# A streamed logsumexp: GpSimd weighs and folds heads of the last units, a fourth head for its bias add in the middle stages, ScalarE's sums of the last tile at the end, and exp(bias) of six heads in PSUM

## The chip, the core and the metric

The kernel runs on one core of a Trainium2 chip. The time is that of the device in microseconds (us); five runs of the kernel before have a median of 329.27 us (328.9 to 329.38). TensorE (PE in the profile), VectorE (DVE), ScalarE (ACT), GpSimd (POOL) and SyncE (SP, which issues the loads) each work through their own queue in order, and wait for one another by semaphores.

## What is computed

x has the shape 8 x 2048 x 2048, 134 MB in float32. Its last axis is split into 8 heads of 256 elements. A bias per head and element is added, and the logsumexp over the 256 elements of each head is written twice (every row of a head is repeated).

```python
x_heads = x.reshape(B, S, H, Dh).transpose(0, 2, 1, 3)
x_heads = x_heads + bias[None, :, None, :]
x_tiled = np.repeat(x_heads, 2, axis=2)
mx = x_tiled.max(axis=-1, keepdims=True)
lse = mx.squeeze(-1) + np.log(np.exp(x_tiled - mx).sum(axis=-1))
```

Both kernels leave out the maximum: they sum exp(x + bias), or exp(x) times exp(bias), and take the logarithm.

## The kernel before, in words

**Tiles and buffers.** The 16,384 rows of x make 64 tiles of 256 rows: 128 partitions with K = 2 rows each, 2 MB a tile. Nine buffers in SBUF hold tiles (NBUF). A load of tile t + 9 is issued by SyncE when all last uses of tile t are done. Most tiles come in one load, the later ones in halves (one of the two rows of each partition, 1 MB), and the two halves of the last tile in three pieces each (LAST_CUTS). "62k1" below means tile 62, second half.

**Three ways for the bias.** For a head, the sum of exp(x + bias) comes about in one of three ways:

- by TensorE: a matmul with bf16 parts of the bias (L193, three rows) and one of x with the identity (L204) add up in a PSUM bank. ScalarE takes exp with its own sum as a side output (`sum_biased`, L223). This costs ScalarE an instruction and an accumulator read for each head.
- by GpSimd: it adds the bias in place (`g_add`, L242), ScalarE takes exp in place (L248), and VectorE sums (L265, in `later`).
- by weights: ScalarE takes exp(x) in place (L248), and VectorE multiplies by exp(bias) and sums. This is either one multiply for several heads (L258) with the reduce at L265, or one custom instruction and an accumulator read for each head (`weigh`, L276), which can start as soon as exp is done.

**Stages.** STAGES gives each tile a mode: `pe` heads go by TensorE, heads from `g0` on by GpSimd, those between by weights. `late` says that the weighted heads wait for GpSimd and use L258; otherwise they are weighed as soon as they have landed. BULK (tiles 0 to 48) has 2 heads by TensorE, 2 by weights, 4 by GpSimd. MIXED (49 to 60, from 57 in halves) has 1, 4 and 3. PROMPT (61 to 63) has 2 by TensorE and 6 by weights; GpSimd has nothing to do there.

**Order.** All engines follow an order written out by hand in the main loop (`tc.manual_schedule`). At each unit of work (a tile, a half or a piece) the loop first issues TensorE's matmuls and GpSimd's add, then what was put off from the unit before: `for_pool` (ScalarE's exp and VectorE's reduce of the heads that GpSimd prepared, and the load of tile t + 9), then the exp of this unit, then `for_pe` (ScalarE's sums of the TensorE heads, in PROMPT put off by one unit), then the weighings. PSUM holds exp(bias) of heads 1 to 4 (w_ps, two banks), five banks for TensorE's sums (ps) and one for transposes. exp(bias) of heads 5 to 7 is in SBUF (w_sb).

**End.** Sums go into R (seven batches) and R_last. After each batch TensorE transposes it (`finish`, L293) and ScalarE takes Ln (L303). One store (L307) writes seven batches; it is issued after all loads. `finish_last` (L314, L320, L321) does the same for the last batch.

Of the kernel before, what the change touches and what calls it, by code (L numbers as in the profile page):

```python
# [19 lines left out]

BULK = dict(pe=2, g0=4, late=True)
MIXED = dict(pe=1, g0=5, late=False)
PROMPT = dict(pe=2, g0=8, late=False)

STAGES = [(0, BULK, False), (49, MIXED, False), (57, MIXED, True), (61, PROMPT, True)]

LAST_CUTS = [[0, 512, 1280, 2048], [0, 512, 1536, 2048]]


@with_exitstack
def kernel(
# [6 lines left out]
    nc = tc.nc  # L40
    P = nc.NUM_PARTITIONS
    B, S, D = x.shape
    H, Dh = bias.shape
    assert D == H * Dh and S % (P * K) == 0
    NBLK = S // (P * K)
    T = B * NBLK
    CPE = 2 * Dh
    MM = 512

    W0, G0, W1 = Dh, 4 * Dh, 5 * Dh  # L50

# [7 lines left out]
    w_sb = sb.tile([P, D - W1], F32, name="w_sb")  # L59
# [9 lines left out]
    res = sb.tile([H * NBLK, B - 1, P, K, 2], F32, name="res")  # L69
    res_last = sb.tile([P, P, 2], F32, name="res_last")  # L70
    xts = [sb.tile([P, K, D], F32, name=f"xt{i}") for i in range(NBUF)]
    w_ps = pp.tile([P, W1 - W0], F32, name="w_ps")
    ps = [pp.tile([P, MM], F32, name=f"ps{i}") for i in range(5)]
    tpair = pp.tile([P, 2, K, P], F32, name="tpair")
    tps = [tpair[:, i] for i in range(2)]

    def mode_of(t):
        return [m for t0, m, _ in STAGES if t0 <= t][-1]

    def halves_of(t):  # L80
        return [s for t0, _, s in STAGES if t0 <= t][-1]

    def pieces(t):

        if not halves_of(t):
            return [(0, K, 0, D)]
        cuts = [[0, D]] * K if t < T - 1 else LAST_CUTS
        return [
            (k, k + 1, c0, c1) for k in range(K) for c0, c1 in zip(cuts[k], cuts[k][1:])
        ]  # L90

    def rows_of(t):

# [79 lines left out]
    for c in range(W0, W1, MM):  # L173
# [5 lines left out]

    n_ps = [0]  # L180

    def add_bias(m, t, k0, k1):


        n = m["pe"] * Dh
        xt = xts[t % NBUF]
        step = MM // n
        groups = [(k, min(k + step, k1)) for k in range(k0, k1, step)]
        got = []
        for ka, kb in groups:  # L190
            p = ps[n_ps[0] % len(ps)]
            n_ps[0] += 1
            nc.tensor.matmul(  # L193
                p[:, 0 : (kb - ka) * n],
                lhsT=ones3,
                rhs=each_row(b3, 0, n, kb - ka),
                start=True,
                stop=False,
            )
            got.append([p[:, k * n : (k + 1) * n] for k in range(kb - ka)])  # L200
        rows = []
        for (ka, kb), views in zip(groups, got):
            p = views[0]
            mm = nc.tensor.matmul(  # L204
                bass.AP(
                    tensor=p.tensor,
                    offset=p.offset,
                    ap=[p.ap[0], [1, (kb - ka) * n]],
                ),
                lhsT=ident,  # L210
                rhs=xt[:, ka:kb, 0:n],
                start=False,
                stop=True,
            )
            on_x(t, mm, [loads[t, k0, 0]])
            rows += [(v, mm) for v in views]
        return rows

    def sum_biased(m, t, k, p, mm, sums):
# [11 lines left out]
    def each_row(src, c, n, k_rows):  # L231

        return bass.AP(
            tensor=src.tensor,
            offset=src.offset + c,
            ap=[src.ap[0], [0, k_rows], [1, n]],
        )

    def g_add(m, t, k0, k1):
        c = m["g0"] * Dh  # L240
        v = xts[t % NBUF][:, k0:k1, c:D]
        add = nc.gpsimd.tensor_tensor(  # L242
            out=v, in0=v, in1=each_row(b_rep, c - G0, D - c, k1 - k0), op=ALU.add
        )
        return on_x(t, add, [loads[t, k0, 0]])

    def exp_inplace(t, v, after):
        return on_x(t, nc.scalar.activation(out=v, in_=v, func=ACT.Exp), [after])  # L248
# [23 lines left out]

    def weigh(t, v, h, dst, after):
        c = h * Dh
        w = w_ps[:, c - W0 : c - W0 + Dh] if c < W1 else w_sb[:, c - W1 : c - W1 + Dh]
        ttr = nc.vector.tensor_tensor_reduce(  # L276
            out=v,
            in0=v,
            in1=w,
            scale=1.0,  # L280
            scalar=0.0,
            op0=ALU.mult,
            op1=ALU.add,
            accum_out=dst,
        )
        last_uses[t].append(on_x(t, ttr, [after]))

    def finish(b):

        nr = H * NBLK  # L290
        tp = tps[b % 2]
        for k in range(K):
            nc.tensor.transpose(  # L293
                out=tp[0:nr, k],
                in_=R[b][:, k].rearrange("p h n -> p (h n)"),
                identity=ident,
            )
# [37 lines left out]
    for_pool = for_pe = None  # L335
    for t in range(T):
        m = mode_of(t)
        xt = xts[t % NBUF]
        sums = sums_of(t)
        for k0, k1, c0, c1 in pieces(t):  # L340
            add = None
            if c0 == 0:
                got = add_bias(m, t, k0, k1)
                if m["g0"] < H:
                    add = g_add(m, t, k0, k1)
            if for_pool:
                for_pool()
                for_pool = None
            h0 = max(c0 // Dh, m["pe"])
            h1 = min(c1 // Dh, m["g0"])  # L350
            if h0 < h1 and not m["late"]:
                done = exp_inplace(
                    t, xt[:, k0:k1, h0 * Dh : h1 * Dh], loads[t, k0, c0]
                )
# [24 lines left out]
            for_pool = pool_part  # L379
            if c0 == 0:  # L380
                if m["g0"] < H:
                    pe_part()
                else:
                    for_pe = pe_part
# [40 lines left out]
```

The softmax here doesn't subtract the row's maximum and nothing guards it: scores larger than these inputs give would overflow.

## Time and profile before

| what | value |
|---|---|
| median of five runs | 329.27 us |
| the profiled execution | 329.14 us |
| its span | 327.4 us |
| VectorE busy | 288.5 us (88%) |
| ScalarE busy | 277.9 us (85%) |
| GpSimd busy | 270.8 us (83%) |
| TensorE busy | 234.2 us (72%) |
| HBM read | 134.23 MB, 413 GB/s over the span |
| share of the chain that ended last | DMA 66%, DVE 16%, POOL 8%, ACT 7% |

The span is what the profiler saw from first to last instruction; the device time is a little longer. A busy share is a mean over the whole span. The chain is followed back from the last instruction to what released it, so its shares say what stood on the path, not what was busy. A load's landing is seen in the profile when the engines that wait for it start. Of single instructions the table below has the means that are used later (duration of one; the next may start some 0.07 to 0.09 us before the end of the one ahead).

| line, engine, what | elements per partition | mean us |
|---|---|---|
| L242 GpSimd bias add | 768, 1536, 2048 | 1.815, 3.451, 4.540 |
| L265 VectorE reduce | 768, 1536, 3072 | 0.948, 1.748, 3.354 |
| L276 VectorE weighing, w in PSUM | 256 | 0.414 |
| L276 VectorE weighing, w in SBUF | 256 | 0.420 |
| L248 ScalarE exp | 512, 768, 1024, 1536 | 0.654, 0.845, 1.055, 1.481 |
| L223 ScalarE exp with sum | 256 | 0.403, and 0.227 for the accumulator read |

### The profile page before, as it was taken

How to read it: one execution, taken by the hardware profiler on the slowest of the kernel's cores; microseconds unless marked ns; L12 is line 12 of the kernel's file. 1: busy time of each engine (PE TensorE's matmuls, PEld its weight loads, DVE VectorE, ACT ScalarE, POOL GpSimd, SP SyncE). 2: the span in 40 equal slices, each digit the busy share in tenths (PEclk: the TensorE clock that was granted, in tenths of full speed). 3: DMA queues.
4: the chain of work that ended last, by engine and by line, in shares of the span. 5: the costliest groups of instructions: out<-in, count | busy, mean ns of one | idle time of the engine just before them, and what ended most of it. 6: DMA issues, size and time to landing. Idle time of an engine off the chain costs nothing.

```text
span 327.4 us, 1988 instructions
## 1 busy us (share of the span) xinstructions
PE 234.2 (72%) x383; PEld 67.5 (21%) x383; DVE 288.5 (88%) x380; ACT 277.9 (85%) x567; POOL 270.8 (83%) x79
## 2 busy tenths in 40 slices
PE   5497869697668797767767689669938446476791
PEld 2032212132212222211221222222202101122220
DVE  0009999999999999999999999989998999999995
ACT  3269999599999889889889888888888998899884
POOL 6999999979999999999999999999989667697400
PEclk9999765559697658778778955885695555555567
DMA  7999999999999999999999999999999999999991
GB/s 289 437 426 428 431 426 432 422 426 434 422 432 427 424 432 423 428 434 420 433 426 421 433 424 428 430 424 432 426 425 436 422 430 417 422 419 419 422 396 52
DMA packets 11646, 135.41 MB, mean 414 GB/s; under 512 B 1329, under 2 KB 1457, under 8 KB 2673
## 3 DMA queue, kind: packets, MB, share of 16 engines
q1 hardware_dynamic: 11536, 135.27, 97.9%
q8 instruction: 3, 0.05, 0.1%
q14 instruction: 9, 0.07, 0.1%
q10 hardware_dynamic: 2, 0.01, 0.0%
q0 software_dynamic: 96, 0.00, 0.0%
HBM read 134.23 MB, written 1.05 MB: 413 GB/s over the span
## 4 chain that ended last, share of the span: by engine, by line
DMA 66%; DVE 16%; POOL 8%; ACT 7%; PE 2%; issue 0%; SPq 0%; DVEq 0%
DMA xt<-in_x_dram 63%; DVE R L265 11%; POOL xt L242 7%; ACT xt L248 6%; DVE xt L258 4%; DMA b<-bparts 2%; PE ps L204 1%; ACT xt L223 1%; DMA brow<-in_bias_dram 1%; DVE xt L276 1%; POOL brest L157 0%; POOL brest L155 0%; PE ps L193 0%; POOL b L160 0%; POOL bparts L156 0%
## 5 line engine op out<-in xcount | busy, mean ns | idle before, releaser
L242 POOL TENSOR_TENSOR xt<-xt,b_rep 128x2048 f32<-128x2048 f32 (+2 forms) x65 | 264.5, 4070 | 33.0 <-DMA xt<-in_x_dram 33.0
L204 PE MATMUL ps<-xt,ident 128*128 128x512 f32 (+1 forms) x240 | 180.0, 884 | 70.5 <-DMA xt<-in_x_dram 69.7
L248 ACT ACTIVATE xt<-xt 128x3072 f32<-128x3072 f32 (+3 forms) x89 | 186.3, 2115 | 15.9 <-POOL xt L242 13.6
L265 DVE TENSOR_REDUCE R<-xt 128x12 f32<-128x3072 f32 (+1 forms) x56 | 176.6, 3154 | 1.7
L223 ACT ACTIVATE xt<-ps 128x256 f32<-128x256 f32 x232 | 87.0, 403 | 17.9 <-PE ps L204 17.7
L258 DVE TENSOR_TENSOR xt<-xt,w_ps 128x1024 f32<-128x1024 f32 x49 | 59.7, 1218 | 32.2 <-ACT xt L248 32.0
L204 PEld LDWEIGHTS ps<-xt,ident 128*128 128x128 f32 x240 | 55.3, 260 | 150.9 <-DMA xt<-in_x_dram 108.2
L193 PE MATMUL ps<-b,ones 3*128 3x512 bf16 (+1 forms) x120 | 48.9, 475 | 6.7 <-DMA b<-bparts 4.0
L223 ACT ACTIVATION_READ_ACCUMULATOR xt<-ps 128x1 f32 x232 | 51.8, 227 | 0.0
L276 DVE CUSTOM_DVE_ANT_0 xt<-xt,w_ps 128x256 f32<-128x256 f32 x114 | 40.5, 414 | 0.3 <-ACT xt L248 0.3
L193 PEld LDWEIGHTS <-ones 3*128 3x128 bf16 x120 | 7.8, 97 | 81.0 <-issue 81.0
L265 DVE TENSOR_REDUCE R_last<-xt 128x3 f32<-128x768 f32 (+1 forms) x9 | 9.3, 1037 | 0.0
L293 PE MATMUL tpair<-ident,R 128*64 128x128 f32 x14 | 3.6, 350 | 4.9 <-DVE R L265 4.9
L276 DVE CUSTOM_DVE_ANT_0 xt<-xt,w_sb 128x256 f32<-128x256 f32 x18 | 6.7, 420 | 0.0
L303 ACT ACTIVATE res<-tpair 64x512 f32<-64x512 f32 x7 | 4.1, 584 | 2.6 <-PE tpair L293 2.6
L164 PE MATMUL ps<-brow,ones 1*128 1x512 f32 x4 | 3.7, 1089 | 3.5 <-DMA brow<-in_bias_dram 3.5
L276 DVE DVE_READ_ACCUMULATOR2_ANT R_last<- 128x1 f32 x76 | 6.2, 82 | 0.0
L170 ACT ACTIVATE b_rep<-ps 128x512 f32<-128x512 f32 x2 | 1.2, 597 | 4.7 <-PE ps L164 4.7
L276 DVE DVE_READ_ACCUMULATOR2_ANT R<- 128x1 f32 x56 | 4.5, 81 | 0.0
L164 PE MATMUL w_ps<-brow,ones 1*128 1x512 f32 x4 | 4.0, 1096 | 0.7 <-ACT w_ps L176 0.7
L293 PEld LDWEIGHTS tpair<-ident,R 128*64 128x64 f32 x14 | 1.8, 147 | 12.1 <-DVE R L265 9.1
L176 ACT ACTIVATE w_ps<-w_ps 128x512 f32<-128x512 f32 x2 | 1.2, 582 | 3.3 <-PE w_ps L164 3.3
(21 smaller groups left out, 12.4 us busy)
## 6 DMA issues: line engine op xcount, KB each, us to landing
xt<-in_x_dram SPq DMA_DIRECT2D x57, 2048.0 KB, 31.9
xt<-in_x_dram SPq DMA_DIRECT2D x12, 1024.0 KB, 24.7
out_dram<-res SPq DMA_DIRECT2D x1, 896.0 KB, 9.8
xt<-in_x_dram SPq DMA_DIRECT2D x3, 256.0 KB, 14.4
xt<-in_x_dram SPq DMA_DIRECT2D x2, 384.0 KB, 16.1
xt<-in_x_dram SPq DMA_DIRECT2D x1, 512.0 KB, 12.3
out_dram<-res_last SPq DMA_DIRECT2D x1, 128.0 KB, 1.7
b<-bparts POOLq DMA_DIRECT2D x3, 1.0 KB, 5.9
```

The lines of the kernel that those rows point to most:

```text
L164: nc.tensor.matmul(dst, lhsT=ones, rhs=brow[:, c0:c1], start=True, stop=True)
L170: nc.scalar.activation(out=b_rep[:, c - G0 : c - G0 + MM], in_=ps[i], func=ACT.Copy)
L193: nc.tensor.matmul(p[:, 0 : (kb - ka) * n], lhsT=ones3, rhs=each_row(b3, 0, n, kb - ka), start=True, stop=False,)
L204: mm = nc.tensor.matmul(bass.AP(tensor=p.tensor, offset=p.offset, ap=[p.ap[0], [1, (kb - ka) * n]],), lhsT=ident, rhs=xt[:, ka:kb, 0:n], s ...
L223: act = nc.scalar.activation(out=xts[t % NBUF][:, k, c : c + Dh], in_=p[:, c : c + Dh], func=ACT.Exp, accum_out=sums[:, k, h : h + 1],)
L242: add = nc.gpsimd.tensor_tensor(out=v, in0=v, in1=each_row(b_rep, c - G0, D - c, k1 - k0), op=ALU.add)
L248: return on_x(t, nc.scalar.activation(out=v, in_=v, func=ACT.Exp), [after])
L258: mul = nc.vector.tensor_tensor(out=f, in0=f, in1=each_row(w_ps, h0 * Dh - W0, n, k1 - k0), op=ALU.mult,)
L265: red = nc.vector.tensor_reduce(out=sums[:, k0:k1, h0:H], in_=v.rearrange("p k (h j) -> p k h j", j=Dh), op=ALU.add, axis=mybir.AxisListTy ...
L276: ttr = nc.vector.tensor_tensor_reduce(out=v, in0=v, in1=w, scale=1.0, scalar=0.0, op0=ALU.mult, op1=ALU.add, accum_out=dst,)
L293: nc.tensor.transpose(out=tp[0:nr, k], in_=R[b][:, k].rearrange("p h n -> p (h n)"), identity=ident,)
L303: nc.scalar.activation(out=res[:, b], in_=tv, func=ACT.Ln)
```

## The change

Five things are edited together.

1. In the last units GpSimd takes over heads from VectorE. The new function `fold` multiplies one or two heads by exp(bias) from SBUF in place, and adds halves onto each other until 32 elements a head are left: four GpSimd instructions, each waiting for the one before. VectorE then only sums 32 elements a head. Half 62k1 folds one head (7), half 63k0 two (6 and 7): three heads in all. The reduce of 62k1's fold stands in VectorE's order after the five weighings of 62k1 and ahead of all of tile 63; that of 63k0 stands at the very end.
2. MIXED has g0 = 4 for 5: GpSimd adds the bias of four heads, VectorE weighs three for four. MIXED starts at tile 50 for 49, and halves start at tile 56 for 57.
3. The last tile is cut into seven pieces for six, in another order, and ScalarE's sums of its TensorE heads (63k0, 63k1) come after all exps of the tile.
4. exp(bias) of heads 1 to 6 lies in PSUM (three banks for two), so TensorE's sums have four banks for five; w_sb holds heads 6 and 7.
5. The bias matmul of a unit is written one unit ahead (`put_bias`, `add_x`).

`fold`, `put_bias` and `add_x` are new; `add_bias` goes. The core of the diff:

```diff
-BULK = dict(pe=2, g0=4, late=True)
-MIXED = dict(pe=1, g0=5, late=False)
-PROMPT = dict(pe=2, g0=8, late=False)
-
-STAGES = [(0, BULK, False), (49, MIXED, False), (57, MIXED, True), (61, PROMPT, True)]
-
-LAST_CUTS = [[0, 512, 1280, 2048], [0, 512, 1536, 2048]]
+BULK = dict(pe=2, g0=4, late=True, fold=0)
+MIXED = dict(pe=1, g0=4, late=False, fold=0)
+PROMPT = dict(pe=2, g0=8, late=False, fold=0)
+PROMPT_F1 = dict(pe=2, g0=8, late=False, fold=1)
+PROMPT_F2 = dict(pe=2, g0=8, late=False, fold=2)
+FOLD = 32
+
+STAGES = [
+    (0, (BULK,)),
+    (50, (MIXED,)),
+    (56, (MIXED, MIXED)),
+    (61, (PROMPT, PROMPT)),
+    (62, (PROMPT, PROMPT_F1)),
+    (63, (PROMPT_F2, PROMPT)),
+]
+
+LAST_COLS = [
+    [(0, 512), (1280, 2048), (512, 1280)],
+    [(0, 512), (512, 1024), (1024, 1536), (1536, 2048)],
+]
...
-    W0, G0, W1 = Dh, 4 * Dh, 5 * Dh
+    W0, G0, W1, W2 = Dh, 4 * Dh, 6 * Dh, 7 * Dh
...
-    w_ps = pp.tile([P, W1 - W0], F32, name="w_ps")
-    ps = [pp.tile([P, MM], F32, name=f"ps{i}") for i in range(5)]
+    w_ps = pp.tile([P, W2 - W0], F32, name="w_ps")
+    ps = [pp.tile([P, MM], F32, name=f"ps{i}") for i in range(4)]
...
+    def fold(t, k, h0, h1, sums, after):
+        v = xts[t % NBUF][:, k, h0 * Dh : h1 * Dh]
+        done = nc.gpsimd.tensor_tensor(
+            out=v, in0=v, in1=w_sb[:, h0 * Dh - W1 : h1 * Dh - W1], op=ALU.mult
+        )
+        on_x(t, done, [after])
+        v = v.rearrange("p (h j) -> p h j", j=Dh)
+        n = Dh
+        while n > FOLD:
+            n //= 2
+            done = nc.gpsimd.tensor_tensor(
+                out=v[:, :, 0:n], in0=v[:, :, 0:n], in1=v[:, :, n : 2 * n], op=ALU.add
+            )
+            on_x(t, done, [])
+
+        def add_up():
+            red = nc.vector.tensor_reduce(
+                out=sums[:, k, h0:h1],
+                in_=v[:, :, 0:FOLD],
+                op=ALU.add,
+                axis=mybir.AxisListType.X,
+            )
+            on_x(t, red, [done])
+
+        return add_up
...
-                got = add_bias(m, t, k0, k1)
+                got = add_x(m, t, k0, bias_there)
+                if next_units:
+                    bias_there = put_bias(*next_units.pop(0))
...
-            if for_pool:
-                for_pool()
-                for_pool = None
+            if c0 == 0 and (t < T - 1 or k0 == 0):
+                flush(for_pool)
             h0 = max(c0 // Dh, m["pe"])
             h1 = min(c1 // Dh, m["g0"])
+            hf = max(h0, min(h1, H - m["fold"]))
             if h0 < h1 and not m["late"]:
                 done = exp_inplace(
                     t, xt[:, k0:k1, h0 * Dh : h1 * Dh], loads[t, k0, c0]
                 )
-            if for_pe and (c0 == 0 or c1 == D):
-                for_pe()
-                for_pe = None
+                if hf < h1:
+                    for_pool.append(fold(t, k0, hf, h1, sums, done))
+            if c0 == 0 and (t < T - 1 or k0 == 0):
+                flush(for_pe)
             if not m["late"]:
                 for k in range(k0, k1):
-                    for h in range(h0, h1):
+                    for h in range(h0, hf):
...
-    for_pe and for_pe()
+    flush(for_pe)
+    flush(for_pool)
     finish_last()
```

In VectorE's queue this makes 320 rows for 382; in GpSimd's it adds eight small instructions behind the last bias add.

More of the change, by code (lines that the diff above doesn't have):

```diff
@@ L71, with modes_of @@
     xts = [sb.tile([P, K, D], F32, name=f"xt{i}") for i in range(NBUF)]
-    w_ps = pp.tile([P, W1 - W0], F32, name="w_ps")
-    ps = [pp.tile([P, MM], F32, name=f"ps{i}") for i in range(5)]
+    w_ps = pp.tile([P, W2 - W0], F32, name="w_ps")
+    ps = [pp.tile([P, MM], F32, name=f"ps{i}") for i in range(4)]
     tpair = pp.tile([P, 2, K, P], F32, name="tpair")
     tps = [tpair[:, i] for i in range(2)]
[L77 to L81, printed above, removed]
+    def modes_of(t):
+        return [modes for t0, modes in STAGES if t0 <= t][-1]
     def pieces(t):
-        if not halves_of(t):
+        if len(modes_of(t)) == 1:
             return [(0, K, 0, D)]
[L87 to L90, printed above, removed]
+        cols = [[(0, D)]] * K if t < T - 1 else LAST_COLS
+        return [(k, k + 1, c0, c1) for k in range(K) for c0, c1 in cols[k]]
     def rows_of(t):
@@ L172 @@
         )
-    for c in range(W0, W1, MM):
+    for c in range(W0, W2, MM):
         w = w_ps[:, c - W0 : c - W0 + MM]
@@ L180, with put_bias @@
     n_ps = [0]
-    def add_bias(m, t, k0, k1):
+    def put_bias(m, k0, k1):
         n = m["pe"] * Dh
-        xt = xts[t % NBUF]
         step = MM // n
-        groups = [(k, min(k + step, k1)) for k in range(k0, k1, step)]
         got = []
-        for ka, kb in groups:
-            p = ps[n_ps[0] % len(ps)]
+        for ka in range(k0, k1, step):
+            kb = min(ka + step, k1)
+            p = ps[n_ps[0] % len(ps)][:, 0 : (kb - ka) * n]
             n_ps[0] += 1
             nc.tensor.matmul(
-                p[:, 0 : (kb - ka) * n],
+                p,
                 lhsT=ones3,
@@ L199, in add_bias, with add_x @@
             )
-            got.append([p[:, k * n : (k + 1) * n] for k in range(kb - ka)])
+            got.append((ka, kb, p))
+        return got
+    def add_x(m, t, k0, got):
+        n = m["pe"] * Dh
         rows = []
-        for (ka, kb), views in zip(groups, got):
-            p = views[0]
+        for ka, kb, p in got:
             mm = nc.tensor.matmul(
[L205 to L209, printed above, removed]
+                p,
                 lhsT=ident,
-                rhs=xt[:, ka:kb, 0:n],
+                rhs=xts[t % NBUF][:, ka:kb, 0:n],
                 start=False,
@@ L215, in add_bias @@
             on_x(t, mm, [loads[t, k0, 0]])
-            rows += [(v, mm) for v in views]
+            rows += [(p[:, k * n : (k + 1) * n], mm) for k in range(kb - ka)]
         return rows
@@ L274, in weigh @@
         c = h * Dh
-        w = w_ps[:, c - W0 : c - W0 + Dh] if c < W1 else w_sb[:, c - W1 : c - W1 + Dh]
+        w = w_ps[:, c - W0 : c - W0 + Dh] if c < W2 else w_sb[:, c - W1 : c - W1 + Dh]
         ttr = nc.vector.tensor_tensor_reduce(
@@ L332, in sums_of, with flush @@
         return R_last[:, :, blk, :].rearrange("p h k -> p k h")
-    for_pool = for_pe = None
+    for_pool = []
+    for_pe = []
+    next_units = [
+        (modes_of(t)[k0], k0, k1)
+        for t in range(T)
+        for k0, k1, c0, _ in pieces(t)
+        if c0 == 0
+    ]
+    bias_there = put_bias(*next_units.pop(0))
+    def flush(later_work):
+        for f in later_work:
+            f()
+        later_work.clear()
     for t in range(T):
-        m = mode_of(t)
         xt = xts[t % NBUF]
@@ L340 @@
         for k0, k1, c0, c1 in pieces(t):
+            m = modes_of(t)[k0]
             add = None
             if c0 == 0:
-                got = add_bias(m, t, k0, k1)
+                got = add_x(m, t, k0, bias_there)
+                if next_units:
+                    bias_there = put_bias(*next_units.pop(0))
                 if m["g0"] < H:
                     add = g_add(m, t, k0, k1)
-            if for_pool:
-                for_pool()
-                for_pool = None
+            if c0 == 0 and (t < T - 1 or k0 == 0):
+                flush(for_pool)
             h0 = max(c0 // Dh, m["pe"])
             h1 = min(c1 // Dh, m["g0"])
+            hf = max(h0, min(h1, H - m["fold"]))
             if h0 < h1 and not m["late"]:
@@ L377, in pe_part @@
                     sum_biased(m, t, k, *got[k - k0], sums)
-            for_pool = pool_part
+            for_pool.append(pool_part)
             if c0 == 0:
@@ L383 @@
                 else:
-                    for_pe = pe_part
+                    for_pe.append(pe_part)
         fb, at = divmod(t - 2, NBLK)
```

## The prediction

> **What bounds the kernel now.** I read the page's DMA rows first, then busy time by stretch, then the timeline of the last 20 us, because a stream that is full until its end leaves only the tail to win.
>
> ```profile
> DMA  7999999999999999999999999999999999999991
> ...
> q1 hardware_dynamic: 11536, 135.27, 97.9%
> ...
> q14 instruction: 9, 0.07, 0.1%
> ```
>
> The loads keep the 16 DMA engines busy from the second slice to the last but one; q1 alone takes 97.9% of the span. The 134.23 MB of x cannot come sooner by any edit of compute, so a gain must lie after the stream, or in its last transfers. q14 carries instruction fetches; I come back to it.
>
> ```profile
> 285.00:310.00 25.00, 17.96 (x33) 6.40 (x33) 25.00 (x102) 23.00 (x42) 17.91 (x9) 0.50 1.01 420
> 310.00:316.80 6.80, 6.61 (x9) 1.66 (x8) 6.80 (x36) 5.82 (x12) 0.00 (x0) 0.50 1.02 401
> 316.80:323.60 6.80, 3.14 (x7) 0.78 (x6) 6.48 (x38) 5.82 (x20) 0.00 (x0) 0.99 0.46 180
> ```
>
> Columns: stretch, length, busy us of PE, PE loads, VectorE, ScalarE, GpSimd, clock, DMA share, GB/s. VectorE has no gap from 285 to 316.8, and only 0.3 us in the last stretch. GpSimd does nothing after 307.
>
> ```profile
> 309.89 1.48 ACT L248 ACTIVATE xt<-xt 128x1536 f32<-128x1536 f32 x1 [0.86 <-DMA xt<-in_x_dram]
> ...
> 312.73 1.48 ACT L248 ACTIVATE xt<-xt 128x1536 f32<-128x1536 f32 x1 [0.63 <-DMA xt<-in_x_dram]
> ...
> 315.29 1.48 ACT L248 ACTIVATE xt<-xt 128x1536 f32<-128x1536 f32 x1 [0.35 <-DMA xt<-in_x_dram]
> ...
> 316.83 0.42 DVE L276 CUSTOM_DVE_ANT_0 xt<-xt,w_ps 128x256 f32<-128x256 f32 x1
> ...
> 318.11 1.59 ACT L248 ACTIVATE xt<-xt 128x768 f32<-128x768 f32 x2
> ...
> 321.41 0.42 DVE L276 CUSTOM_DVE_ANT_0 xt<-xt,w_ps 128x256 f32<-128x256 f32 x1 [0.26 <-ACT xt L248]
> ...
> 323.48 0.08 DVE L276 DVE_READ_ACCUMULATOR2_ANT R_last<- 128x1 f32 x1
> ...
> 323.70 0.45 PE L314 MATMUL tpair<-ident,R_last 128*128 128x128 f32 x1 [3.76 <-DVE R_last L276]
> ```
>
> ScalarE waits for the landing of 61k1, 62k0 and 62k1 (tile, half) at 309.9, 312.7 and 315.3. VectorE reaches 62k1 at 316.83, just after its exp (315.29+1.48=316.77): from here on it is no longer behind. Then it has 18 weighings and one wait of 0.3 us for ScalarE, and ends at 323.56. From there to the span's end are 3.84 us (transpose, Ln, store, close), which the change leaves alone.
>
> [...] After the change GpSimd works at the end while VectorE weighs heads 2 to 6 from PSUM; head 7, from SBUF, comes only when no fold runs. [...] after an 8 KB fetch on q14 that starts at 310.02 (309 to 329 ns each), one packet of x takes 968 ns, where others of 8 KB take 313. [...] the q14 packets here are 8 KB.
>
> **The change, part by part.**
>
> *Setup.* One more bank of exp(bias): a matmul of 1.09 us and an exp of 0.58, less 0.2 on w_sb. ScalarE then sits idle 5.6 us before its first sum (18.69), which waits for TensorE and b3. That idle time covers it: nothing; without it 1.5 us, which the full stream takes up.
>
> *Bias ahead.* TensorE's own order stays bias, x, bias, x. With four banks for five, the bias of a tile waits for the sums of two tiles before, done some 4.9 us earlier. Nothing.
>
> *Middle stages.* Stage by landing pace (4.9 us a tile, 2.485 a half). VectorE before: 8 weighings x 0.342 + 1.67 = 4.40 a tile. After: 6 x 0.342 + a reduce of 2048 elements. Reduces of 768, 1536, 3072 take 948, 1748, 3354 ns, so 1.042 ns an element: 2.21 as pitch, 4.26 in all; a half 2.16 for 2.23. But tile 49 stays BULK (4.5 us, and its reduce ends 0.5 us later: 262.6 for 262.1). Then 6 x 4.26 and 10 x 2.155 put the start of 61k0 at 309.7, not 310.65: about 0.9 us of margin, which ends at the landing of 62k1. Worth nothing by itself. GpSimd takes 1024 elements a half: 0.18 + 2.13 ns each (from 1815, 3451, 4540 ns) = 2.36 of 2.485. It fits with 0.1 to spare; if it overran by 0.1 a half, ten halves cost 1 us of that margin. ScalarE uses 2.04 of 2.485.
>
> *SyncE.* Two more loads (tile 56 in halves, seven last pieces for six), 0.33 us of issue each, while SyncE waits. Each load also waits for the landing of the eighth before it (the last went out at 309.88, the eighth before it, 61k1, landed at 309.86). So the last 256 KB go out when 62k0 has landed (312.7; before 309.9), and the store of res when 62k1 has (315.3; before 312.77). From there to the last landing (320.35) 7.6 and 5 us of x are still ahead in the queues; cost nothing, and C if that cover fails. The added small packets (2 KB at 84 ns, 4 KB at 165): 8 rows a DMA engine x 3 ns, nothing.
>
> *ScalarE's tail.* Same work in another order: exps first, sums at the end. From 316.68: 4 sums x 0.357 to 318.11, two exps of 768 at 0.735 to 319.58, three of 512 at 0.52 (1536 takes 1.39 of pitch, two of 768 1.47: 0.08 fixed) to 321.14, four sums to 322.6. Before 322.6 too. The last piece, landed 320.35, is due at 320.62: 0.27 spare.
>
> *GpSimd folds.* 62k1, one head: mult 256, adds 128, 64, 32: 4 x 0.18 + 480 x 2.13 ns = 1.75, and four hand-offs of 0.07 (gaps in the bias chain at 4 to 7 us): 2.0. Small shapes are not in the trace: from below 1.2 (fixed part 0.05, as the 1x512 subtraction of 1.14 has), from above 3.0 (0.3 fixed, 0.25 a hand-off). I take 2.0. Queued behind it on VectorE is a reduce of 32, then all of tile 63. 63k0, two heads: 0.72 + 960 x 2.13 ns + 0.28 = 3.05, from 318.9 to 321.95; due at 322.77.
>
> *VectorE's tail.* From 316.8: five weighings to 318.51; wait for the fold (318.85); reduce 0.10 (0.1 to 0.25); head 5 of 63k0 to 319.29; heads 2 to 4 wait for their exp (319.65) and end at 320.71; 63k1 three pairs, all exps done before (320.2, 320.75, 321.3), to 322.77; reduce of 64 elements, 0.14: 322.95. So 0.6 us before 323.56: three weighings (1.03) and the 0.3 of waiting go, 0.7 of new waits and reduces come.
>
> *The fetch.* Three q14 fetches (124.06, 276.77, 310.02) come when 48, 179 and 310 VectorE instructions have started: every 131. The third falls where the landing of 62k0 is 0.37 late (309.86 to 312.71, where halves come every 2.485) and 62k1 0.07 more. The change takes 62 rows off VectorE, so its 310th instruction comes at about 320.5, as the last x lands. I take 0.4 us off both landings and the whole tail; bounds 0 (another DMA engine is as late) and 0.45. VectorE's margin of 0.9 pays for it.
>
> **Sum.** Against the profiled execution (329.14, span 327.4): 323.56 to 322.55, 1.0 us less (case A: 0.6 of work, 0.4 of fetch). The five runs have a median of 329.27, 0.13 above it; from there **328.27**.
>
> **Rivals.**
> *B, the landing stays*: only the 0.6 of work: 328.66. For it: twelve fetches lie in the span (nine on q14, three on q8), and I attribute the third by its spacing. Against: the 0.37 falls on it.
> *C, the last landing moves*: if the last piece, issued 3 us later than its like before, lands at 321.55 rather than 320.35, ScalarE ends at 321.57+0.52+1.43=323.5, and nothing is won: 329.2. Against: 5 us of queue stand before it.
> *D, slower: the first fold stalls VectorE.* Its reduce stands in front of ten weighings. VectorE ends at 322.95 plus what the fold takes over 2.4 us (there the wait for exp covers it). With 3.0 us the gain is gone; with 3.6 the end is 324.15: 329.87. For it: no small GpSimd operation on 128 partitions that hands to the next is in the trace. Against: a 128x128 memset takes 204 ns.
>
> **Chances.** A 0.54, B 0.26, C 0.09, D 0.11. A measurement tells 0.2%, 0.66 us, from no change, so faster means under 328.61. A gives 0.51 faster and 0.03 same (a fold at its upper bound), B lies on the line (0.13 and 0.13), C same, D slower: 0.64, 0.25, 0.11. A's own range is 328.0 to 328.9: below, the 0.24 by which five runs of one kernel differ; above, a fold of 3.0 us (0.6). A shorter fold wins nothing, since VectorE then waits for the exp. With B whole and most of C, 327.8 to 329.2 holds about 0.85.
>
> **What would show it.** ScalarE's exp of 62k1 starts near 314.9, not 315.29 (A) or stays (B). GpSimd's first fold lasts 2.0 us and VectorE waits under 0.5 us for it (D: over 1). VectorE waits 0.4 to 0.9 us before 62k1. The chain ends with VectorE's reduce, ScalarE's last sum 0.3 us before it. Wrong if a DMA wait at the end, or GpSimd, stands last, or if middle tiles lose pace.

## The result and the profile after

| | before | after |
|---|---|---|
| median of the runs, us | 329.15 (328.73 to 329.55, 38 runs) | 328.30 (327.85 to 328.65, 20 runs) |
| profiled execution, us (span) | 329.14 (327.4) | 328.16 (326.4) |

The ratio is 0.9974, with a 95% interval of 0.9968 to 0.998: 0.85 us faster, for a forecast of 328.27. So the number held, but not all the steps under it. One run each of e3 (518.5 us) and e9 (516.7 us) took far longer than all others and is left out of the medians below. Sums below are made in the profiled executions.

The first view is the page of after:

```profile
span 326.4 us, 1959 instructions
...
DMA  7999999999999999999999999999999999999993
...
q1 hardware_dynamic: 11696, 135.27, 98.4%
...
q14 instruction: 10, 0.08, 0.1%
```

The stream is as full as before, and q14, which the page names "instruction", has one fetch more inside the span: its last are at 318.46 and 321.41, where before has 310.02 and then 328.37, past its span. The second view is busy time by stretch (columns as before):

```profile
285.00:310.00 25.00, 17.31 (x33) 6.28 (x33) 24.55 (x79) 24.14 (x43) 22.82 (x10) 0.50 1.01 420
310.00:316.50 6.50, 6.50 (x8) 1.58 (x8) 6.50 (x38) 6.22 (x14) 0.15 (x1) 0.50 1.02 399
316.50:322.80 6.30, 4.30 (x7) 0.99 (x6) 5.69 (x34) 6.04 (x21) 4.45 (x8) 0.77 0.71 219
```

VectorE executes 79 instructions for 102 in the first stretch and still has only 0.45 us of idle time there. In the last stretch GpSimd works 4.45 us where it did nothing, VectorE has 0.6 us of gaps, and ScalarE is idle for 0.26 only. The third view is the timeline, with one line from the middle stages and the tail:

```profile
286.60 2.29 DVE L274 TENSOR_REDUCE R<-xt 128x8 f32<-128x2048 f32 x1 [0.45 <-ACT xt L257]
...
310.32 0.42 DVE L285 CUSTOM_DVE_ANT_0 xt<-xt,w_ps 128x256 f32<-128x256 f32 x1
...
312.30 1.48 ACT L257 ACTIVATE xt<-xt 128x1536 f32<-128x1536 f32 x1
...
314.79 1.48 ACT L257 ACTIVATE xt<-xt 128x1536 f32<-128x1536 f32 x1 [0.28 <-DMA xt<-in_x_dram]
...
316.35 0.79 POOL L301 TENSOR_TENSOR xt<-xt,w_sb 128x256 f32<-128x256 f32 x1 [8.53 <-ACT xt L257]
...
316.48 0.42 DVE L285 CUSTOM_DVE_ANT_0 xt<-xt,w_ps 128x256 f32<-128x256 f32 x1
...
317.22 1.18 POOL L309 TENSOR_TENSOR xt<-xt 128x128 f32<-128x128 f32 x3
...
317.81 3.49 ACT L257 ACTIVATE xt<-xt 128x768 f32<-128x768 f32 x5
...
318.44 0.18 DVE L315 TENSOR_REDUCE R_last<-xt 128x1 f32<-128x32 f32 x1 [0.16 <-POOL xt L309]
...
318.73 1.28 POOL L301 TENSOR_TENSOR xt<-xt,w_sb 128x512 f32<-128x512 f32 x1 [0.33 <-ACT xt L257]
...
319.42 0.42 DVE L285 CUSTOM_DVE_ANT_0 xt<-xt,w_ps 128x256 f32<-128x256 f32 x1 [0.30 <-ACT xt L257]
...
320.08 1.66 POOL L309 TENSOR_TENSOR xt<-xt 128x256 f32<-128x256 f32 x3
...
322.50 0.22 DVE L315 TENSOR_REDUCE R_last<-xt 128x2 f32<-128x64 f32 x1
322.54 0.22 ACT L232 ACTIVATION_READ_ACCUMULATOR xt<-ps 128x1 f32 x1
```

The exp of 62k1 starts at 314.79, half a us earlier. The first fold lasts from 316.35 to 318.40 (2.05 us), the second from 318.73 to 321.74 (3.01). VectorE waits 0.16 for the first and 0.30 for the exp of heads 2 to 4. VectorE (322.72) and ScalarE (322.76) end together. The chain of waits, each row with its start and length, says what ScalarE waited for:

```profile
309.81 10.19 DMA xt<-in_x_dram
320.01 0.02 issue
320.03 0.63 ACT xt L257
320.66 0.01 issue
320.67 0.63 ACT xt L257
321.30 1.46 ACT xt L232 x8
```

The last two exps start on the landings of their pieces (320.01 and 320.65), and only then come the four sums. A transfer, not VectorE, now leads to the end, which the prediction had named as a sign that it would be wrong.

Where the time went follows from the landings (from the transfers' own records in the trace) and from the later end of the two engines:

| us | before | after | change |
|---|---|---|---|
| 61k1 lands | 309.86 | 309.80 | -0.06 |
| from there to the landing of 62k1 | 5.41 | 4.97 | -0.44 |
| from there to the last end | 8.29 | 7.99 | -0.30 |
| last end | 323.56 | 322.76 | -0.80 |

In the table of experiments below, these two intervals are called the *gap* and the *tail*; the tail is given for VectorE and ScalarE apart.

### The profile page after: what moved, and what is told of

It is laid out like the page before. It is cut to its first block, busy times and chain, and to the rows that moved or that the text cites. A ratio compares the mean times of both kernels' runs of the same rounds, so it can differ in the third digit from the quotient of the medians.

```text
span 326.4 us, 1959 instructions
## 1 busy us (share of the span) xinstructions
PE 232.2 (71%) x391; PEld 67.4 (21%) x391; DVE 285.9 (88%) x318; ACT 278.1 (85%) x574; POOL 288.3 (88%) x88
## 4 chain that ended last, share of the span: by engine, by line
DMA 69%; DVE 15%; ACT 6%; POOL 6%; PE 3%; issue 0%; SPq 0%
DMA xt<-in_x_dram 66%; DVE R L274 11%; ACT xt L257 4%; POOL xt L251 4%; DVE xt L267 4%; PE ps L217 2%; DMA b<-bparts 2%; ACT xt L232 1%; DMA brow<-in_bias_dram 0%; POOL brest L167 0%; POOL brest L165 0%; POOL b L170 0%; PE ps L202 0%; POOL bparts L164 0%; POOL bparts L166 0%
## 5 line engine op out<-in xcount | busy, mean ns | idle before, releaser
L251 POOL TENSOR_TENSOR xt<-xt,b_rep 128x2048 f32<-128x2048 f32 (+1 forms) x66 | 277.4, 4208 | 22.1 <-DMA xt<-in_x_dram 21.8
L217 PE MATMUL ps<-xt,ident 128*128 128x512 f32 (+1 forms) x244 | 177.0, 858 | 80.1 <-DMA xt<-in_x_dram 79.9
L274 DVE TENSOR_REDUCE R<-xt 128x12 f32<-128x3072 f32 (+1 forms) x56 | 181.4, 3240 | 2.2 <-ACT xt L257 0.4
L202 PE MATMUL ps<-b,ones 3*128 3x512 bf16 (+1 forms) x122 | 47.6, 457 | 3.3 <-ACT xt L232 2.4
L285 DVE CUSTOM_DVE_ANT_0 xt<-xt,w_ps 128x256 f32<-128x256 f32 x95 | 34.0, 416 | 0.4 <-ACT xt L257 0.3
L274 DVE TENSOR_REDUCE R_last<-xt 128x4 f32<-128x1024 f32 x10 | 12.2, 1216 | 0.0
L301 POOL TENSOR_TENSOR xt<-xt,w_sb 128x256 f32<-128x256 f32 (+1 forms) x2 | 2.1, 1032 | 8.9 <-ACT xt L257 8.9
L174 PE MATMUL w_ps<-brow,ones 1*128 1x512 f32 x6 | 6.0, 1108 | 1.3 <-ACT w_ps L186 1.3
L285 DVE DVE_READ_ACCUMULATOR2_ANT R<- 128x1 f32 x36 | 3.0, 82 | 0.0
L309 POOL TENSOR_TENSOR xt<-xt 128x128 f32<-128x128 f32 (+3 forms) x6 | 2.5, 422 | 0.5
```

What stands on the lines that cost most here:

```text
L174: nc.tensor.matmul(dst, lhsT=ones, rhs=brow[:, c0:c1], start=True, stop=True)
L202: nc.tensor.matmul(p, lhsT=ones3, rhs=each_row(b3, 0, n, kb - ka), start=True, stop=False,)
L217: mm = nc.tensor.matmul(p, lhsT=ident, rhs=xts[t % NBUF][:, ka:kb, 0:n], start=False, stop=True,)
L251: add = nc.gpsimd.tensor_tensor(out=v, in0=v, in1=each_row(b_rep, c - G0, D - c, k1 - k0), op=ALU.add)
L274: red = nc.vector.tensor_reduce(out=sums[:, k0:k1, h0:H], in_=v.rearrange("p k (h j) -> p k h j", j=Dh), op=ALU.add, axis=mybir.AxisListTy ...
L285: ttr = nc.vector.tensor_tensor_reduce(out=v, in0=v, in1=w, scale=1.0, scalar=0.0, op0=ALU.mult, op1=ALU.add, accum_out=dst,)
```

## The experiments

Two theories were to be told apart: that the gain comes from the landings (the fetch), or from the work taken off VectorE's tail (folds, order of sums). All kernels start from the kernel after. "Last" is the time from the landing of 62k1 to that of the last piece.

| kernel | median, us | ratio to before | gap | last | tail VectorE | tail ScalarE |
|---|---|---|---|---|---|---|
| before | 329.15 | | 5.41 | 5.08 | 8.29 | 7.35 |
| after | 328.30 | 0.9968 to 0.998 | 4.97 | 5.88 | 7.95 | 7.99 |
| e1_no_fold | 328.44 | 0.9968 to 0.9986 | 4.98 | 5.87 | 7.92 | 7.98 |
| e2_sums_early | 328.33 | 0.9964 to 0.9985 | 5.00 | 5.85 | 8.47 | 7.93 |
| e2b_sums_early | 328.40 | 0.9963 to 0.9984 | 4.97 | 5.87 | 7.98 | 7.44 |
| e3_pad52 | 328.52 | 0.9969 to 0.9989 | - | - | - | - |
| e3b_pad52 | 328.37 | 0.9963 to 0.9983 | 5.50 | 5.37 | 7.79 | 7.94 |
| e4_pad183 | 329.32 | 0.9994 to 1.001 | 5.87 | 5.19 | 7.76 | 7.44 |
| e5_old_middle | 328.40 | 0.9967 to 0.9986 | 5.07 | 5.09 | 7.76 | 7.44 |
| e6_fewer_act | 328.06 | 0.9956 to 0.998 | 4.99 | 5.19 | 7.92 | 7.60 |
| e7_tail | 328.09 | 0.9949 to 0.9974 | 4.98 | 5.18 | 7.28 | 7.44 |
| e9_tail_fewer | 327.95 | 0.995 to 0.9976 | - | - | - | - |
| e9b_tail_fewer | 327.63 | 0.9938 to 0.9963 | 5.03 | 5.13 | 7.29 | 7.44 |
| e10_long_fold | 328.62 | 0.9971 to 0.9986 | 5.00 | 5.87 | 8.20 | 7.98 |

Of e3 and e9 no trace is read; e3b and e9b are the same kernels, run again. Most runs of one kernel lie within 0.5 us of its median. The kernel before ran beside each group, with medians of 329.21 (e1, e2, e3, e4), 329.22 (e5, e6, e7, e9) and 329.34 (e2b, e3b, e9b, e10), so the ratios compare better than the times.

### The folds: e1

```diff
-    (62, (PROMPT, PROMPT_F1)),
-    (63, (PROMPT_F2, PROMPT)),
```

> The changed kernel without folds: VectorE weighs all 18 heads of the last three halves itself. Theory 1 (the waits for ScalarE's exps set VectorE's pace at the end; the folds' work was mostly hidden behind them): VectorE ends about 0.15 us later, 328.3 to 328.5. Theory 2 (the three weighings taken off VectorE are the gain): 3 x 0.343 = 1.03 us less the two reduces of 0.45, so 328.9 or more.

Measured: 328.44, which is 0.14 us more than after and within the scatter. VectorE's tail is 7.92 us for 7.95, and the later of the two ends is the same (7.98 for 7.99). The timeline of e1 shows why (VectorE's weighings from 62k1 on: the first, those before and after the one break, the first of 63k1, and the last):

```profile
316.46 0.41 DVE L283 CUSTOM_DVE_ANT_0 xt<-xt,w_ps 128x256 f32<-128x256 f32 x1
...
318.16 0.42 DVE L283 CUSTOM_DVE_ANT_0 xt<-xt,w_sb 128x256 f32<-128x256 f32 x1
...
318.53 0.42 DVE L283 CUSTOM_DVE_ANT_0 xt<-xt,w_ps 128x256 f32<-128x256 f32 x1
...
320.58 0.41 DVE L283 CUSTOM_DVE_ANT_0 xt<-xt,w_ps 128x256 f32<-128x256 f32 x1
...
322.29 0.42 DVE L283 CUSTOM_DVE_ANT_0 xt<-xt,w_sb 128x256 f32<-128x256 f32 x1
```

From 316.46 to 322.71 all 18 weighings run at a pitch of 0.342 with one gap of 0.03. They need 6.25 us; with three heads folded the 15 weighings, two reduces and two waits need 6.24 (316.48 to 322.72). The folds save three weighings and give them back as waits for GpSimd and ScalarE.

### ScalarE's sums last: e2, e2b

```diff
-            if c0 == 0 and (t < T - 1 or k0 == 0):
+            if c0 == 0 or (c0, c1) == LAST_COLS[k0][-1]:
                 flush(for_pe)
```

> The changed kernel, but ScalarE's sums of 63k0 come right after the two exps of that half, as before, and not at the very end. Theory 1 (exps early are what counts): the three exps of 63k1 move back by 0.7 us, VectorE waits for them and ends about 0.35 us later: 328.65. Theory 2 (only VectorE's work counts): no change, 328.3.

> As e2_sums_early, once more, since its trace showed VectorE's end 0.5 us later after the landing and its times did not: theory 1 wants 8.45 us from the landing of 62k1 to VectorE's end (7.95 in the changed kernel) and 328.6 to 328.8; theory 2 wants 328.3.

Measured: 328.33 and 328.40, no different from after, so the loss that theory 1 foresaw did not show in the medians. But the two traces of this one kernel differ by half a us at VectorE's end, and so do their executions: that of e2 took 329.20, the longest of its eight, that of e2b 328.35. Timeline of e2:

```profile
320.08 0.38 ACT L232 ACTIVATE xt<-ps 128x256 f32<-128x256 f32 x1 [0.22 <-PE ps L217]
...
320.81 1.66 ACT L257 ACTIVATE xt<-xt 128x512 f32<-128x512 f32 x3
...
321.47 0.42 DVE L285 CUSTOM_DVE_ANT_0 xt<-xt,w_ps 128x256 f32<-128x256 f32 x1 [0.46 <-ACT xt L257]
```

and of e2b:

```profile
319.36 0.40 ACT L232 ACTIVATE xt<-ps 128x256 f32<-128x256 f32 x1
...
320.07 1.69 ACT L257 ACTIVATE xt<-xt 128x512 f32<-128x512 f32 x3
```

In e2 the sums of 63k0 wait for TensorE, the exps of 63k1 behind them start 0.74 us later (0.51 when counted from the landing of 62k1), and VectorE waits 0.46 for them. The stretches tell why TensorE was late (the clock is the third column from the right); here is that of e2:

```profile
318.00:319.00 1.00, 1.00 (x2) 0.49 (x2) 0.83 (x7) 1.00 (x4) 0.71 (x3) 0.50 0.99 287
```

and the same one of e2b:

```profile
318.00:319.00 1.00, 1.00 (x4) 0.35 (x3) 0.83 (x6) 1.00 (x3) 0.75 (x3) 1.00 1.00 297
```

With half the clock the two matmuls of 63k0 took 2.06 us in e2, with the full clock 1.13 in e2b. Putting the sums last takes TensorE's clock off VectorE's path. That is seen in these traces; its worth in the median is too small to tell.

e1 and e2b together: either part alone gives VectorE the same end as both. Before had both 18 weighings and a wait for ScalarE. e1 keeps the weighings and has no waits; e2b has waits (0.17, 0.29, 0.22) and three weighings fewer. A kernel without folds *and* with early sums was not run, so that the two replace each other is not shown, and there is a rival that both runs contain: the new cuts of the last tile. In before, VectorE began 63k1 6.14 us after the landing of 62k1 (321.41), in e1 5.78 after it (320.58), and these 0.36 us are nearly the whole difference of the two tails (8.29 and 7.92). It waited there for an exp of 1024 elements, which ScalarE began at 320.29, in this timeline of before:

```profile
320.29 1.60 ACT L248 ACTIVATE xt<-xt 128x1024 f32<-128x1024 f32 x2
```

That is 5.02 us after the landing, as in e2b (320.07). With the new cuts the first exp of 63k1 has 512 elements and takes 0.65 us for 1.06. So by an estimate from these figures it ends 5.67 us after the landing even with early sums, 0.1 before VectorE wants it in e1. The cuts alone may then be enough for VectorE's part of the gain, as long as TensorE is not late as in e2. No run has them alone.

### The fetch: e3, e3b, e4

```diff
     nc.vector.memset(ones3, 1.0)
+    for i in range(52):          # 183 in e4
+        nc.vector.memset(pad[:, i : i + 1], 0.0)
```

> The changed kernel with 52 memsets of one element on VectorE in the setup, where it is idle until 23 us. They move VectorE's third instruction fetch from 321.4 to about 308, where the kernel before had it. Fetch theory (case A): the landings of 62k0 and 62k1 are 0.4 us later again, and the time 0.35 us more, 328.65. Rival B (the landings do not hang on the fetch): 328.3.

> As e3_pad52, once more for its trace: a fetch near 308, and then the landing of 62k1 0.4 us (between 0.1, as in e5, and 0.9, as in e4) more than 4.97 us after that of 61k1; time 328.4 to 328.7. Rival B: 4.97 us and 328.3.

> The same with 183 memsets: VectorE's fetches come four times before 310 us instead of two. Fetch theory: two more fetches of 0.98 us on one DMA engine that is 0.6 us ahead of the last, so the last landings and the time are about 1.3 us later: 329.6. Rival B: 328.3, or what the memsets themselves delay at the start, which the stream hides.

These VectorE instructions, of one element of a new tile `pad` each, run at the start and change nothing in the tail but VectorE's count, and with it the place of VectorE's fetches. Measured: in e3b a q14 fetch falls at 311.35 and the gap is 5.50; in e4 at 311.37, and the gap is 5.87. This is the DMA of e4 by queue (packets, MB, share of 16 engines) from 309.9 to 313.5, about the landing of 61k1 to that of 62k0:

```profile
q1 hardware_dynamic: 358, 1.43, 99.4%
q14 instruction: 1, 0.01, 0.6%
```

and in after, over the like stretch (309.9 to 312.8), there is no q14 row at all:

```profile
q1 hardware_dynamic: 257, 1.20, 101.5%
```

ScalarE's timeline in e4 shows the delay as a wait:

```profile
313.46 1.48 ACT L260 ACTIVATE xt<-xt 128x1536 f32<-128x1536 f32 x1 [0.82 <-DMA xt<-in_x_dram]
...
315.97 1.48 ACT L260 ACTIVATE xt<-xt 128x1536 f32<-128x1536 f32 x1 [0.30 <-DMA xt<-in_x_dram]
```

62k0 landed 3.36 us after 61k1, where 2.485 is the pace. Over the twelve traces that were read there is no exception: the eight without a fetch from 309 to 313 have gaps of 4.97 to 5.03, the four with one 5.07 (e5), 5.41 (before), 5.50 and 5.87.

Why one fetch costs anything from 0.1 to 0.9 can be read from the transfers' records. The trace has sixteen times for each load, the last of which is its landing. I take them for the sixteen DMA engines; the trace does not name them. From 61k1 to 62k0 in after all sixteen step by 2.48 to 2.50 us, so each can be followed. Where a fetch falls, a single one comes late, and the other fifteen keep their steps within 0.06 us:

| trace, fetch at | the late one was ahead of the last by | it came later by | 62k0 landed later than 2.485 us after 61k1 by |
|---|---|---|---|
| e5, 310.23 | 0.97 | 0.99 | 0.02 |
| before, 310.02 | 0.61 | 0.98 | 0.36 |
| e3b, 311.35 | 0.48 | 1.02 | 0.54 |
| e4, 311.37 | 0.10 | 0.97 | 0.88 |

So the fetch holds up one DMA engine by about 1 us, and the landing moves by what exceeds that engine's lead over the slowest. Why the lead was 0.10 in e4 and 0.97 in e5 is not shown.

In time, e4 is clear: 329.32, all of the change's gain gone. Its trace explains two thirds of that: from the landing of 61k1 to the last end it has 13.63 us for 12.96. The rest lies ahead of 61k1, which landed at 310.07 for 309.80; but it landed between 309.79 and 310.28 in the kernels without added instructions too. e3 is not clear: 328.52 and 328.37, intervals that overlap after's. In the trace of e3b the last end comes 13.44 us after the landing of 61k1 (gap and longer tail), for 12.96 in after; but its medians are only 0.22 and 0.07 higher, and the ratios 0.9979 and 0.9973 for 0.9974. So the times confirm a loss for e4 alone.

### The middle stages: e5

```diff
-MIXED = dict(pe=1, g0=4, late=False, fold=0)
+MIXED = dict(pe=1, g0=5, late=False, fold=0)
...
-    (50, (MIXED,)),
-    (56, (MIXED, MIXED)),
+    (49, (MIXED,)),
+    (57, (MIXED, MIXED)),
```

> The changed kernel with the middle stages of before (GpSimd 3 heads, VectorE weighs 4, from tile 49, halves from 57). VectorE has about 70 instructions more, so its third fetch is back near 310. Fetch theory: 62k1 lands 0.4 us later and the time is 328.65 to 328.75. If VectorE's pace in the middle stages had no other effect, e3 and this one give the same.

Measured: 328.40, again within the scatter of after. A fetch came back, at 310.23, but the gap grew by 0.1 only. Another went: the next one comes at 327.21, so that none falls into the last pieces, and the last lands 5.09 us after 62k1 for 5.88 (see e6). ScalarE's page row counts 569 instructions in e5, for 574 in after and 567 in before. So five of the seven that the change adds come from the middle stages: the edit that moved VectorE's fetch out of the stream moved ScalarE's into it. The two nearly cancel here, and the pace of the middle stages is not tested by itself.

### The last pieces: e6

In after, a fetch at 318.46 delays the last two landings: the last but one landed 1.33 us after the piece before it, where about 0.67 is the pace. I count it to ScalarE's row of fetches, which in after come when 46, 183, 310, 438 and 564 of its instructions have started (33.82, 103.62, 171.66, 240.28 and 318.46; seven that the page leaves out are counted here). A count alone does not place the fifth: in before the first four come at 45, 182, 309 and 437, but 564 have started by 320.29 and no fetch comes before 328.37. e6 saves five of ScalarE's instructions, so that the fetch at 318.46 should fall after the stream: one exp over all of w_ps for three, and Ln for two batches at a time.

```diff
-        nc.scalar.activation(out=w, in_=w, func=ACT.Exp)
+    nc.scalar.activation(out=w_ps, in_=w_ps, func=ACT.Exp)
...
+        if b % 2 == 0 and b < B - 2:
+            return
-        nc.scalar.activation(out=res[:, b], in_=tv, func=ACT.Ln)
+        nc.scalar.activation(out=res[:, b0 : b + 1], in_=tv, func=ACT.Ln)
```

> The changed kernel with five ScalarE instructions less (exp(bias) in one instruction for three, Ln of the batches in pairs), so that ScalarE's fetch of 318.46 comes about 321.4, after the stream. Fetch theory: the last two pieces land 0.65 us earlier (320.0 for 320.65) and ScalarE ends 0.4 us earlier, but VectorE, which ends at the same moment, does not: 328.25 to 328.3. Rival (the last landing bounds the end): 327.9.

Measured: no fetch falls between 287.20 and 321.41. The pieces land 0.64 apart, the last 5.19 after 62k1, and ScalarE's tail shrinks to 7.60. VectorE's stays at 7.92 and takes the end over. 328.06 is 0.24 better, which the intervals don't separate from after.

The sixteen times say the same as for VectorE's fetch. ScalarE's holds one of them up by 0.65 to 0.69 us here, where the pieces are smaller. In after, e1, e2, e2b and e10 that one was the last already, and the landing moved by all of it. In e3b (fetch at 319.07) it was 0.52 ahead and cost 0.16, in e4 (319.66) 0.91 ahead and cost nothing.

### A tail in the order of landing: e7, e9, e9b

Since ScalarE and VectorE end together, both have to be shortened. e7 does the exps of tile 63 as the pieces land, with one sum between two exps, and puts the reduce of 62k1's fold behind the weighings of 63k0. e9 and e9b add e6's saving. The cores of the edits:

```diff
-            if c0 == 0 and (t < T - 1 or k0 == 0):
-                flush(for_pool)
+            if t == T - 1 and (k0, c0) == (1, 0):
+                for_pool.pop(0)()
+            elif c0 == 0 and t < T - 1:
+                flush(for_pool)
...
-            if c0 == 0 and (t < T - 1 or k0 == 0):
-                flush(for_pe)
+            if c0 == 0 and (t, k0) < (T - 2, 1):
+                flush(for_pe)
+            elif h0 < h1 and (t, k0) >= (T - 2, 1) and for_pe:
+                for_pe.pop(0)()
...
-                    for_pe.append(pe_part)
+                    for h in range(m["pe"]):
+                        for_pe.append(lambda h=h, f=pe_part: f(h))
```

> A new order of ScalarE's tail: exps of tile 63 as soon as their piece lands, the sums of 62k0, 62k1 and 63 one at a time in between, and the reduce of 62k1's fold behind the weighings of 63k0. VectorE then no longer waits 0.25 us for the fold and 0.3 us for an exp. With the last pieces landing at 320.0 and 320.65: VectorE ends at 322.5, ScalarE at 322.5, 0.2 us less: 328.1. If the waits are not what costs: 328.3.

> The new order of ScalarE's tail together with five ScalarE instructions less. If both bounds hold as read (VectorE waits for exps; the last pieces land late because of ScalarE's fetch), both engines end near 322.1: 0.4 to 0.65 us less, 327.7 to 327.9. If the fetch only moves into the last landing again: 328.1, as the new order alone.

> As e9_tail_fewer, once more for its trace: VectorE's end 7.3 us after the landing of 62k1, ScalarE's about the same, 327.7 to 328.0.

Measured: e7 328.09, with a tail of 7.44 for 7.99, an interval that overlaps after's; e9 327.95 and e9b 327.63. e7 moves ScalarE's fetch as well: with the sums put off, none falls between 287.28 and 320.35, and the last piece lands at 320.31, 5.18 after 62k1. So ScalarE's shorter tail may be due to the fetch, to the order, or to both; VectorE's 7.28 is due to the order, since e6 leaves it at 7.92. Timeline of e9b:

```profile
316.58 0.83 ACT L257 ACTIVATE xt<-xt 128x768 f32<-128x768 f32 x1
...
317.67 0.84 ACT L257 ACTIVATE xt<-xt 128x768 f32<-128x768 f32 x1
...
318.76 0.63 ACT L257 ACTIVATE xt<-xt 128x512 f32<-128x512 f32 x1
...
319.57 0.18 DVE L315 TENSOR_REDUCE R_last<-xt 128x1 f32<-128x32 f32 x1
...
321.89 0.22 DVE L315 TENSOR_REDUCE R_last<-xt 128x2 f32<-128x64 f32 x1
322.01 0.24 ACT L232 ACTIVATION_READ_ACCUMULATOR xt<-ps 128x1 f32 x1
```

The first exp of tile 63 starts at 316.58 (317.81 in after), and the reduce has no wait in front of it. This version has the lowest median: e9b's ratio to before, 0.9951 (0.9938 to 0.9963), lies below all of after's interval, while e9's (0.995 to 0.9976), the same kernel, overlaps it; that it beats before is clear, by how much it beats after is not.

### A longer fold: e10

The fold goes on to 4 elements in the first of the two (three more adds on GpSimd), to put rival D to the test.

```diff
-        while n > FOLD:
+        last = FOLD if t == T - 1 else 4
+        while n > last:
...
-                in_=v[:, :, 0:FOLD],
+                in_=v[:, :, 0:last],
```

> The changed kernel, with the fold of 62k1 carried on to 4 elements (three more GpSimd adds of 16, 8 and 4, about 0.8 us), that of 63k0 as it is. Rival D's mechanism (the fold's reduce stands in front of ten weighings, and what the fold takes over about 2.4 us is paid): fold 2.85 us, VectorE's end after the landing of 62k1 0.4 us later than in the changed kernel (8.35 for 7.95), time near 328.65. If the fold is hidden: 7.95 and 328.3.

Measured: 328.62, with an interval that overlaps after's. In the timeline the reduce stands in VectorE's queue ahead of tile 63 and waits:

```profile
317.52 2.04 POOL L310 TENSOR_TENSOR xt<-xt 128x128 f32<-128x128 f32 x6
...
319.60 0.16 DVE L316 TENSOR_REDUCE R_last<-xt 128x1 f32<-128x4 f32 x1 [1.03 <-POOL xt L310]
```

The fold lasts 2.87 us (316.69 to 319.56), 0.8 more than in after, and VectorE's tail grows by 0.25, to 8.20. The shorter reduce gives 0.18 back: the next weighing follows it after 0.07, in after 0.25.

## Why the prediction was right, and where it was not

**The fetch (0.4).** Right, and for the reason given. The gap shrank by 0.44; VectorE's third fetch left the stream (321.41, at its 312th instruction, for a forecast of 320.5). e3b and e4 brought it back by nothing but a count, and the gap with it. What the prediction had only as a bound ("another DMA engine is as late") is what sets the size: 0.1 to 0.9 us in the gap, by the lead of one DMA engine, and from some 0.1 or 0.2 (e3, e5, within the scatter) to 1.0 us (e4) in the time. Its sign for case A, an exp of 62k1 that starts near 314.9 and not at 315.29, was met (314.79), but it would not have told the cases apart: in e2, where no fetch falls near these landings, that exp starts at 315.30, because 61k1 landed at 310.28. The gap tells them apart.

**The work (0.6).** Half of it: 0.30. Three terms of that sum were off. (1) "VectorE waits 0.4 to 0.9 us before 62k1": it reached that half at 316.48, 0.2 us after the exp's end, and so started 1.71 us after the landing for the 1.53 of the sum: 0.18 lost. The pace of the middle tiles was as forecast (4.24 us for 4.26), but tile 50 began 0.2 late (262.81), there was one wait of 0.45 for ScalarE at the change to halves (tile 56), and 61k0 started at 310.32, not 309.7. The margin that was to pay for the earlier landings went there. (2) VectorE's tail took 6.24 us for 6.15: heads 2 to 4 started 2.94 us after the first weighing, not 2.85. The reduce of 32 took 0.25 of pitch, not 0.10, but that was mostly covered by the wait for the exp. (3) ScalarE ended 0.04 after VectorE, and not 0.3 before it, behind a DMA wait. 0.18 + 0.09 + 0.04 is the missing 0.3.

**"0.27 spare" for the last piece.** This step failed: the piece landed 5.88 us after 62k1 and not 5.08, because the fetch at 318.46 fell into it. The prediction moved VectorE's fetch and did not count ScalarE's instructions, which the change had also moved. It was rival C in small, and with it a transfer stood last in the chain, against the prediction. SyncE's later issues, which C suspected, are not the cause: e6, e7 and e9b keep them, and their last pieces land after 5.13 to 5.19.

**The folds.** 2.05 and 3.01 us for 2.0 and 3.05, so D did not strike. e10 shows that its mechanism is there, and where it decides: a fold of 2.87 cost VectorE 0.25 + 0.18 = 0.43, where the point of 2.4 would have it 0.47. But the sum put the worth of the folds into the 0.6, as "three weighings (1.03)"; e1 shows that without them the end is the same. They remove work that then becomes waiting. In the order of e9b they may be worth something: 18 weighings from its start, 1.62 us after the landing, would end at about 7.86 by their pitch, for 7.29 with folds. That is an estimate; no such run was made.

**Why the time came out at 328.3 all the same.** The traces give 0.80 up to the last end, and 0.84 up to the issue of the last store; the executions differ by 0.98, and the medians by 0.85. The forecast had 1.0. An overestimate of 0.3 in the work was made up in part by 0.1 in the landings (0.44 and 0.06 for 0.4), and the rest is within the scatter of the runs. That 328.27 and 328.30 agree so well is in part luck: the forecast took 1.0 from a median of five runs (329.27) that 38 runs put at 329.15. And the split into 0.44 and 0.30 is that of one execution of each kernel; e3's times do not confirm the 0.44.

**Not tested.** The new cuts of the last tile, the third bank of exp(bias) and the bias matmul written ahead are in every run that starts from after. That the last two are worth nothing, as the prediction has it, is not shown.

## What to carry to other kernels

When a stream fills the span to its end, look at what else shares its DMA engines in the last 10 us: count the instructions of *every* engine between instruction fetches (in after 130 to 134 of VectorE's and 126 to 137 of ScalarE's; near the end one fetch held a DMA engine up by 0.65 to 1.02 us), and see in the trace which fetch the edit moves into or out of the last transfers. Taking work off the engine that ends last gains only as far as nothing else is as late; here ScalarE, held by the last piece, ended within 0.04 us of VectorE, and only runs in which both got shorter (e7, e9b) brought it down by half a us. A margin that is to pay for an earlier landing must be checked for waits between its stage and the end, since the pace alone doesn't give it.

## What the runs showed of the hardware

The instruction fetches showed no wait on the engine they are counted to (VectorE is busy 6.80 of the 6.80 us from 310.00 to 316.80 in before, with its fetch at 310.02, and ScalarE 1.00 of 1.00 from 318 to 319 in after, with its fetch at 318.46), but they showed in the landings: the fetch at 310.02 in before and that at 318.46 in after each held up landings (by 0.4 and 0.65 us), and 52 or 183 instructions of one element at the start of VectorE's program moved a landing 310 us later by 0.5 and 0.9 us.

TensorE's granted clock rose from 0.50 to 1.00 at different times in two executions of one kernel (after 319 in e2, by 317 in e2b), and a pair of matmuls took 2.06 or 1.13 us accordingly.

GpSimd's small operations were dearer than their elements: 128x32 took 250 ns, 128x64 319, 128x128 455 (fixed part about 0.18 us, an estimate from these at the 2.13 ns an element of the large bias adds), with 0.07 to 0.08 us from one to the next. VectorE's weighings from PSUM kept their pitch of 0.342 while a fold ran (316.48 to 317.85 in after).

The prediction expected no weighing of head 7, which has both inputs in SBUF, while a fold runs. One came: in eight of the ten traces with folds, that of head 7 of 62k0 overlapped the first multiply of the fold, and in e5 wholly:

```profile
316.78 1.01 POOL L301 TENSOR_TENSOR xt<-xt,w_sb 128x256 f32<-128x256 f32 x1 [9.72 <-ACT xt L257]
316.79 0.42 DVE L285 CUSTOM_DVE_ANT_0 xt<-xt,w_sb 128x256 f32<-128x256 f32 x1
```

GpSimd paid for it, the more the longer the two overlapped. The multiply took 728 and 732 ns without overlap (e4, e3b), 732 to 789 ns with 0.11 to 0.20 us of it (789 in after), and 1012 ns with 0.42 us, while VectorE's weighing kept its 0.42 us. So a slowdown that the prediction did not price is seen here; it cost the folds under 0.1 us in after (789 ns for 732).
